# Seven block products in place of eight in half of the chunks of a gate and up projection

## The chip, the core and the metric

The kernel runs on one core of one Trainium2 chip. A core has a matrix engine (TensorE, PE in the rows, with PEld for its weight loads), VectorE (DVE), ScalarE (ACT), GpSimd (POOL) and the DMA queues, SP's among them. The metric is device time in microseconds for one execution; lower is better.

## The reference, cut to what matters

The reference is one layer of a streaming encoder for 256 tokens of width 2048: four token mixers merged by gates, then a feed-forward block (SwiGLU). The change lies in the feed-forward block alone:

```python
h = rms_norm(x, norm_ffn_pre[l])
ffn = (jax.nn.silu(h @ w_gate[l]) * (h @ w_up[l])) @ w_down[l]
x = x + rms_norm(ffn, norm_ffn_post[l])
```

`h` is 256 x 2048, `w_gate` and `w_up` are 2048 x 5632, `w_down` is 5632 x 2048, all float32.

## The kernel before, in words

Each float32 matrix product is computed as three products of rounded operands. Both factors are split into a high part in the engine's float32r format and a low part, the rest; then hi·hi, hi·lo and lo·hi are added up in PSUM. The activations are split once and stay in SBUF with their 2048 features on 16 x 128 partitions (`h2_hi`, `h2_lo`; the trace calls them `h_hi`, `h_lo` or, by their buffers, `hT_hi`, `hT_lo`). The weights stream through.

A weight chunk holds 256 input features and 512 output columns, 512 KB, as a tile of 128 partitions x 2 x 512. `Stream.chunk` (L587 to L601) loads it through SP's queue into one of four `raw` buffers, ScalarE writes the rounded high part `hi` (L599), and VectorE subtracts it from `raw` into `lo` (L600); `hi` and `lo` have three buffers each. These steps carry a raised priority, so that the program's scheduler lets them run ahead of the products.

`gemm_tok` (L645 to L663) takes eight chunks for one group of 512 columns. Each chunk has two halves `k` of 128 features; each of them meets two halves `i` of 128 tokens in three matmuls (L660 to L662), with 128 x 128 activations as the stationary operand and 512 weight columns moving, so 12 matmuls a chunk. The sum for each half of the tokens fills one PSUM bank of 512 columns. The first stages of the kernel use `gemm_feat` (L668 to L682) in its place, where the weights are stationary and 256 activation columns move, 24 matmuls a chunk.

The feed-forward part (L1012 to L1034) runs over 11 groups `g` of 512 columns: the gate product into two banks `bg`, then ScalarE's sigmoid (L1024) and VectorE's scaled product (L1025) out of those banks into `sg`, the up product into two banks `bu`, the multiplication by `bu` (L1028), eight transposes on TensorE into `tq` (L1033) and two copies into `aT` (L1034), from which the down projection reads. In the program, the first operands of the down projection are made by L1043 and L1044 (`ah`, `al`). Each engine takes its instructions in the order in which the scheduler wrote them; a waiting instruction holds up what is queued behind it on its engine. GpSimd has no part in the eleven groups; it issues the load of the gain vector `gain2` (L1016) ahead of them, and elsewhere it writes constants, issues a few loads and computes inverse square roots with a power operation (L157, L337, L379, L643, L729).

Of the kernel before, what the change touches and what calls it, by code (L numbers as in the profile page):

```python
# [6 lines left out]
F32 = mybir.dt.float32  # L7
F32R = mybir.dt.float32r
I32 = mybir.dt.int32
AF = mybir.ActivationFunctionType  # L10
ALU = mybir.AluOpType
AX = mybir.AxisListType
PSUM = bass.MemoryType.PSUM
# [567 lines left out]
class Stream:  # L581


    def __init__(self, e, ring):
        self.e, self.ring = e, ring
# [18 lines left out]
def hybrid_kernel(tc, x, xt, w_l, w_in, w_branch, w_out, w_gate, w_up, w_down, post_mix, post_ffn, wa2_d, w2_d, a2_d, g2_d, lq_d,  # L604
# [9 lines left out]
    with ExitStack() as ctx:  # L614
# [4 lines left out]
        e.dram = ctx.enter_context(tc.tile_pool(name="dr", bufs=1, space=bass.MemoryType.DRAM))  # L619
        mmp = ctx.enter_context(tc.tile_pool(name="mmp", bufs=1, space=PSUM))  # L620
        stream = Stream(e, ring)

        def bank():
            return mmp.tile([128, 512], F32, tag="mm", name="mm", bufs=4)
# [15 lines left out]
        def rms(ssum, n, eps):  # L640

            V.tensor_scalar(ssum, ssum, 1.0 / n, eps, op0=ALU.mult, op1=ALU.add)  # L642
            G.tensor_tensor(ssum, ssum, e.mhalf.to_broadcast(list(ssum.shape)), op=ALU.pow)  # L643

        def gemm_tok(w, lhs, nk, banks, runs={}, into={}):  # L645

# [18 lines left out]
        def columns(w, g):  # L665
            return lambda kc: w[kc, g]
# [345 lines left out]
        with ExitStack() as fctx:  # L1012
            F = fctx.enter_context(tc.tile_pool(name="F", bufs=1))
            aT = F.tile([128, 44, 256], F32, name="aT")
            gain = F.tile([128, 2048], F32, name="gain2")
            nc.gpsimd.dma_start(gain, post_ffn.unsqueeze(0).to_broadcast([128, 2048]))  # L1016
            with tc.tile_pool(name="tq", bufs=1, space=PSUM) as tq:
                for g in range(11):
                    bg, bu = [bank(), bank()], [bank(), bank()]
                    lhs2 = lambda kt: (h2_hi[:, kt], h2_lo[:, kt])  # L1020
                    sg = F.tile([128, 2, 512], F32, tag="sg", name="sg", bufs=2)
                    gemm_tok(columns(w_gate, g), lhs2, 16, bg, {0: 3} if g == 0 else {})
                    for i in range(2):
                        S.activation(sg[:, i], bg[i], AF.Sigmoid, scale=r2[:, i, 0:1])  # L1024
                        V.scalar_tensor_tensor(sg[:, i], bg[i], r2[:, i, 1:2], sg[:, i], op0=ALU.mult, op1=ALU.mult)  # L1025
                    gemm_tok(columns(w_up, g), lhs2, 16, bu)
                    for i in range(2):
                        V.tensor_tensor(sg[:, i], sg[:, i], bu[i], op=ALU.mult)  # L1028
                    for kp in range(2):
                        ps = tq.tile([128, 2, 256], F32, tag="tq", name="tq", bufs=4)  # L1030
                        for k in range(2):
                            for i in range(2):
                                T.transpose(ps[:, k, i * 128:(i + 1) * 128], sg[:, i, (2 * kp + k) * 128:(2 * kp + k + 1) * 128], ident)  # L1033
                        S.copy(aT[:, 4 * g + 2 * kp:4 * g + 2 * kp + 2], ps)  # L1034
            wd = fctx.enter_context(tc.tile_pool(name="wd", bufs=1, space=PSUM))
            fg = F.tile([128, 2, 2048], F32, name="fg")
            sq = F.tile([128, 512], F32, name="sqf", bufs=2)
# [51 lines left out]
            for i in range(2):  # L1089
                with tc.high_priority(offset=e.boost):  # L1090
                    V.tensor_reduce(s1[:, i:i + 1], ssq[:, i], axis=AX.X, op=ALU.add)
                    rms(s1[:, i:i + 1], 2048.0, 1e-6)
                for g in range(4):
                    cs = slice(g * 512, (g + 1) * 512)
                    V.scalar_tensor_tensor(fg[:, i, cs], fg[:, i, cs], s1[:, i:i + 1], x2[:, i, cs], op0=ALU.mult, op1=ALU.add)
                    (nc.sync, nc.scalar)[g % 2 * i].dma_start(outr[:, i, cs], fg[:, i, cs])


class TagPool:
# [67 lines left out]
```

## Time and profile before

| | us |
|---|---|
| median of 3 runs (lowest to highest) | 1647.84 (1646.72 to 1647.86) |
| the profiled execution, device time | 1646.59 |
| its span in the trace | 1644.8 |
| TensorE with a matmul in flight | 1630.7 |
| VectorE busy | 996.4 |
| ScalarE busy | 760.4 |
| GpSimd busy | 33.1 |

Busy times are read against the span, and by stage: the average of the whole span mixes stages with different loads. A matmul's row lasts longer than its place in the stream, since matmuls overlap; the time that one costs is the distance from its start to the next one's. A row's last bracket says how long its engine was idle before it and what ended that.

### The profile page before, as it was taken

Reading aid. Unit: us, or ns where it says so; the run is one execution under the profiler, and the core shown is the slowest. Engines: PE = TensorE matmul, PEld = TensorE weight load, DVE = VectorE, ACT = ScalarE, POOL = GpSimd, SP = SyncE. Lnnn points to the kernel's source line nnn. Section 1 sums busy time; section 2 is a strip of 40 time slices with the busy share of each in tenths; the row PEclk is TensorE's granted clock in tenths of the full one; section 3 lists DMA queues with packets and bytes.
Section 4 is the critical chain, followed back from the end, with each engine's and each line's share of the span. In section 5 each row is a group of like instructions: output and inputs, shape, how many; then the busy total and the mean of one; then the engine's idle time right before and its main releaser. Section 6 shows DMA issues by size and latency. Waiting matters only on the chain.

```text
span 1644.8 us, 21807 instructions
## 1 busy us (share of the span) xinstructions
PE 1630.7 (99%) x8632; PEld 1384.1 (84%) x8632; DVE 996.4 (61%) x1173; ACT 760.4 (46%) x879; POOL 33.1 (2%) x46
## 2 busy tenths in 40 slices
PE   9999999999999999999999999999999999999997
PEld 8999988887889978888888888888888888888886
DVE  7668785669875477555555755554455555556555
ACT  6453443336554355444444644444444444445443
POOL 0000110000000001000000000000000000000000
PEclk9999999999999999999999999999999999999999
DMA  8554565445556545765655555555555555555564
GB/s 296 182 167 145 185 205 177 138 141 166 167 167 193 186 160 182 267 192 190 184 190 203 190 188 188 190 192 189 187 189 190 192 193 189 185 198 188 200 192 141
DMA packets 85974, 306.84 MB, mean 187 GB/s; under 512 B 9584, under 2 KB 11904, under 8 KB 85360
## 3 DMA queue, kind: packets, MB, share of 16 engines
q1 hardware_dynamic: 84208, 298.72, 55.7%
q0 software_dynamic: 1232, 5.95, 1.1%
q8 instruction: 67, 1.10, 0.3%
q10 hardware_dynamic: 432, 0.79, 0.1%
q14 instruction: 35, 0.29, 0.0%
HBM read 302.40 MB, written 3.01 MB: 186 GB/s over the span
## 4 chain that ended last, share of the span: by engine, by line
PE 97%; DVE 1%; issue 1%; DMA 0%; ACT 0%; POOL 0%; DVEq 0%; POOLq 0%; ACTq 0%
PE mm L661 21%; PE mm L662 21%; PE mm L660 21%; PE mm L682 4%; PE mm L680 4%; PE mm L681 4%; PE mm L1055 2%; PE mm L1057 2%; PE mm L1056 2%; PE wd L1057 2%; PE wd L1055 2%; PE wd L1056 2%; PE tq L1033 1%; DVE lo L600 0%; PE ps L464 0%
## 5 line engine op out<-in xcount | busy, mean ns | idle before, releaser
L600 DVE TENSOR_TENSOR lo<-raw,hi 128x1024 fp32r<-128x1024 f32 (+1 forms) x554 | 676.9, 1223 | 552.0 <-ACT hi L599 550.8
L599 ACT CAST hi<-raw 128x1024 fp32r<-128x1024 f32 (+1 forms) x554 | 582.4, 1051 | 723.3 <-PE mm L662 510.3
L661 PE MATMUL mm<-lo,h_hi 128*128 128x512 f32 x704 | 274.9, 390 | 0.0
L662 PE MATMUL mm<-hi,h_lo 128*128 128x512 f32 x704 | 273.9, 390 | 0.1
L660 PE MATMUL mm<-hi,h_hi 128*128 128x512 f32 x704 | 250.6, 391 | 0.2 <-ACT h_hi L360 0.2
L661 PE MATMUL mm<-lo,hT_hi 128*128 128x512 f32 x608 | 238.7, 393 | 0.2 <-DVE lo L600 0.2
L662 PE MATMUL mm<-hi,hT_lo 128*128 128x512 f32 x608 | 237.6, 391 | 0.0
L660 PE MATMUL mm<-hi,hT_hi 128*128 128x512 f32 x608 | 219.7, 392 | 1.9 <-ACT vg L894 1.9
L681 PE MATMUL mm<-hT_lo,hi 128*128 128x256 f32 (+1 forms) x640 | 179.9, 282 | 0.7 <-DVE hT_lo L361 0.7
L682 PE MATMUL mm<-hT_hi,lo 128*128 128x256 f32 (+2 forms) x640 | 178.6, 283 | 1.2 <-DVE lo L600 1.2
L680 PE MATMUL mm<-hT_hi,hi 128*128 128x256 f32 (+1 forms) x640 | 179.7, 283 | 0.0
L660 PEld LDWEIGHTS mm<-hi,h_hi 128*128 128x128 f32 x704 | 132.2, 188 | 27.8 <-ACT h_hi L360 0.9
L662 PEld LDWEIGHTS mm<-hi,h_lo 128*128 128x128 f32 x704 | 132.2, 188 | 27.6 <-DVE s L642 0.5
L661 PEld LDWEIGHTS mm<-lo,h_hi 128*128 128x128 f32 x704 | 132.2, 188 | 27.0
L660 PEld LDWEIGHTS mm<-hi,hT_hi 128*128 128x128 f32 x608 | 114.2, 188 | 26.2 <-ACT vg L894 2.3
L661 PEld LDWEIGHTS mm<-lo,hT_hi 128*128 128x128 f32 x608 | 114.2, 188 | 25.0 <-issue 1.0
L662 PEld LDWEIGHTS mm<-hi,hT_lo 128*128 128x128 f32 x608 | 114.2, 188 | 23.8 <-issue 0.3
L682 PEld LDWEIGHTS mm<-hT_hi,lo 128*128 128x128 f32 (+2 forms) x640 | 119.7, 188 | 2.5 <-DVE lo L600 1.6
L681 PEld LDWEIGHTS mm<-hT_lo,hi 128*128 128x128 f32 (+1 forms) x640 | 120.2, 188 | 1.6 <-DVE hT_lo L361 0.9
L680 PEld LDWEIGHTS mm<-hT_hi,hi 128*128 128x128 f32 (+1 forms) x640 | 119.6, 187 | 1.1 <-issue 0.2
L1057 PE MATMUL mm<-hi,al 128*128 128x512 f32 x168 | 65.4, 389 | 0.0
L1056 PE MATMUL mm<-lo,ah 128*128 128x512 f32 x168 | 65.4, 389 | 0.0
(361 smaller groups left out, 1672.4 us busy)
## 6 DMA issues: line engine op xcount, KB each, us to landing
raw<-in_w_in_dram SPq DMA_DIRECT2D x224, 512.0 KB, 3.5
raw<-in_w_gate_dram SPq DMA_DIRECT2D x88, 512.0 KB, 3.5
raw<-in_w_up_dram SPq DMA_DIRECT2D x88, 512.0 KB, 3.5
raw<-in_w_down_dram SPq DMA_DIRECT2D x88, 512.0 KB, 3.4
raw<-in_w_branch_dram SPq DMA_DIRECT2D x32, 512.0 KB, 3.8
raw<-in_w_out_dram SPq DMA_DIRECT2D x32, 512.0 KB, 3.5
raw<-in_w_l_dram SPq DMA_DIRECT2D x8, 464.0 KB, 7.4
xs<-in_x_dram POOLq DMA_DIRECT2D x1, 2048.0 KB, 12.1
```

What stands on the lines that cost most here:

```text
L599: nc.scalar.copy(hi[:, :, :w], raw[:, :, :w])
L600: nc.vector.tensor_tensor(lo[:, :, :w], raw[:, :, :w], hi[:, :, :w].bitcast(F32), op=ALU.subtract)
L660: mm(banks[i_], ah[:, ts], hi[:, k, :], start=kt == 0, stop=False)
L661: mm(banks[i_], ah[:, ts], lo[:, k, :], start=False, stop=False)
L662: mm(banks[i_], al[:, ts], hi[:, k, :], start=False, stop=kt == nk - 1)
L680: mm(ps, hi[:, k, cs], hT_hi[:, kt, :], start=first, stop=False, skip_group_check=True)
L681: mm(ps, hi[:, k, cs], hT_lo[:, kt, :], start=False, stop=False, skip_group_check=True)
L682: mm(ps, lo[:, k, cs], hT_hi[:, kt, :], start=False, stop=last, skip_group_check=True)
L1033: T.transpose(ps[:, k, i * 128:(i + 1) * 128], sg[:, i, (2 * kp + k) * 128:(2 * kp + k + 1) * 128], ident)
L1055: mm(bk[j][i], ah[:, k, ts], hi[:, k, :], start=kt == 0, stop=False)
L1056: mm(bk[j][i], ah[:, k, ts], lo[:, k, :], start=False, stop=False)
L1057: mm(bk[j][i], al[:, k, ts], hi[:, k, :], start=False, stop=kt == 43)
```

## The change

In the gate and up products four of the eight chunks (numbers 1, 3, 4 and 6) are multiplied in another way; the first gate product stays as it was. Such a chunk is seen as a product of 2 x 2 blocks: two halves of the tokens by two halves of the features, and two halves of the features by two halves of 256 columns. The plain way takes eight block products, Strassen's scheme in Winograd's form takes seven, of sums of the blocks.

- Sums of activation blocks (`Seven.sums`): once, four sums for each of the four chunks, on GpSimd, split into high and low by ScalarE and VectorE.
- Sums of weight blocks (`Seven.chunk`): for each such chunk GpSimd makes four blocks of 256 columns in three additions. ScalarE and VectorE then split seven blocks, three loaded ones and four sums, with two instructions each where there was one.
- The products (`Seven.products`): seven blocks of 256 columns, three matmuls each. Three products fall into one token half's columns alone and are added up in the product's own banks; the other four go to two extra banks `px` and `py`, one buffer each.
- The closing (`Seven.close`): once per product, ScalarE copies a half bank, and five VectorE instructions combine `px` and `py` and add the product's own banks into an SBUF tile `w7` with one buffer. The sigmoid, the scaled product and the multiplication read that tile in place of the banks.
- Room: `tq` has two buffers in place of four, and `gain2`, its load and the pool of the down projection's tiles come after the weight blocks' pool has ended.

The core of the diff:

```diff
+        def gemm_seven(w, lhs, banks, seven):
+            px, py = seven.banks()
+            for kc in range(8):
+                if kc in seven.kcs:
+                    seven.products(kc, lhs, seven.chunk(w(kc)), banks, px, py, kc == seven.kcs[0])
+                    continue
+                hi, lo = stream.chunk(w(kc))
...
+            with tc.high_priority(offset=e.boost):
+                return seven.close(banks, px, py)
...
+                seven = Seven(e, U, tq, (1, 3, 4, 6))
                 for g in range(11):
...
-                    gemm_tok(columns(w_gate, g), lhs2, 16, bg, {0: 3} if g == 0 else {})
+                    if g == 0:
+                        gemm_tok(columns(w_gate, g), lhs2, 16, bg, {0: 3})
+                        zg = bg
+                        seven.sums(h2_hi, h2_lo)
+                    else:
+                        zg = gemm_seven(columns(w_gate, g), lhs2, bg, seven)
...
-                    gemm_tok(columns(w_up, g), lhs2, 16, bu)
+                    zu = gemm_seven(columns(w_up, g), lhs2, bu, seven)
                     for i in range(2):
-                        V.tensor_tensor(sg[:, i], sg[:, i], bu[i], op=ALU.mult)
+                        V.tensor_tensor(sg[:, i], sg[:, i], zu[i], op=ALU.mult)
                     for kp in range(2):
-                        ps = tq.tile([128, 2, 256], F32, tag="tq", name="tq", bufs=4)
+                        ps = tq.tile([128, 2, 256], F32, tag="tq", name="tq", bufs=2)
...
+    def sums(self, h_hi, h_lo):
+        for c, kc in enumerate(self.kcs):
+            t = self.pool.tile([128, 4, 256], F32, tag="t", name="t", bufs=2)
...
+            G.tensor_tensor(h, h_hi[:, 2 * kc:2 * kc + 2].bitcast(F32), h_lo[:, 2 * kc:2 * kc + 2].bitcast(F32), op=ALU.add)
...
+            nc.scalar.copy(self.s_hi[:, c], s)
+            nc.vector.tensor_tensor(self.s_lo[:, c], s, self.s_hi[:, c].bitcast(F32), op=ALU.subtract)
+    def chunk(self, ap):
+        with e.tc.high_priority(offset=e.boost):
+            raw = e.ring.tile([128, 2, 512], F32, tag="raw", name="raw", bufs=e.nraw)
+            nc.sync.dma_start(raw, ap)
+            b = raw.rearrange("p k (c n) -> p (k c) n", c=2)
+            t = self.pool.tile([128, 4, 256], F32, tag="t", name="t", bufs=2)
+            G.tensor_tensor(t[:, 0:2], b[:, 1:3], b[:, 0:1].to_broadcast([128, 2, 256]), op=ALU.add)
+            G.tensor_tensor(t[:, 2], t[:, 0], b[:, 2], op=ALU.add)
+            G.tensor_tensor(t[:, 3], t[:, 2], b[:, 3], op=ALU.add)
+            hi, lo = (self.pool.tile([128, 1920], F32R, tag=n, name=n, bufs=2)[:, 48:1840].rearrange("p (b n) -> p b n", n=256)
+                      for n in ("hi7", "lo7"))
+            for x, o in ((b[:, 1:4], slice(0, 3)), (t, slice(3, 7))):
+                nc.scalar.copy(hi[:, o], x)
+                nc.vector.tensor_tensor(lo[:, o], x, hi[:, o].bitcast(F32), op=ALU.subtract)
+    def products(self, kc, lhs, ch, banks, px, py, first):
...
+        for (ah, al), b, ps, st in ((a(0, 0), 0, px[:, 0], first), (s(1), 5, px[:, 1], False), (s(2), 4, py[:, 0], first),
+                                    (s(0), 3, py[:, 1], False), (a(1, 0), 2, banks[0][:, 256:512], False),
+                                    (s(3), 1, banks[0][:, 0:256], False), (a(1, 1), 6, banks[1][:, 256:512], False)):
+            mm(ps, ah, hi[:, b], start=st, stop=False, skip_group_check=True)
+            mm(ps, ah, lo[:, b], start=False, stop=False, skip_group_check=True)
+            mm(ps, al, hi[:, b], start=False, stop=kc == self.kcs[-1], skip_group_check=True)
+    def close(self, banks, px, py):
+        w = self.pool.tile([128, 5, 256], F32, tag="w7", name="w7", bufs=1)
+        nc.scalar.copy(w[:, 2], px[:, 0])
+        V.tensor_tensor(w[:, 0], w[:, 2], px[:, 1], op=ALU.add)
+        V.tensor_tensor(w[:, 4], w[:, 0], py[:, 0], op=ALU.add)
+        V.tensor_tensor(w[:, 1:4:2], py[:, 1:2].to_broadcast([128, 2, 256]), w[:, 0:5:4], op=ALU.subtract)
+        for i in range(2):
+            o = w[:, 1 + 2 * i:3 + 2 * i].rearrange("p b n -> p (b n)")
+            V.tensor_tensor(o, o, banks[i], op=ALU.add)
```

## Rows read from the trace of the kernel before

**Rows 1.** Page, part 1: engine, busy us (share of span), instructions; last, granted clock by slices.

```profile
PE 1630.7 (99%) x8632; PEld 1384.1 (84%) x8632; DVE 996.4 (61%) x1173; ACT 760.4 (46%) x879; POOL 33.1 (2%) x46
...
PEclk9999999999999999999999999999999999999999
```

**Rows 2.** Page, part 4: shares of the chain that ended last, by engine and line.

```profile
PE 97%; DVE 1%; issue 1%; DMA 0%; ACT 0%; POOL 0%; DVEq 0%; POOLq 0%; ACTq 0%
PE mm L661 21%; PE mm L662 21%; PE mm L660 21%; PE mm L682 4%; PE mm L680 4%; PE mm L681 4%; PE mm L1055 2%; PE mm L1057 2%; PE mm L1056 2%; PE wd L1057 2%; PE wd L1055 2%; PE wd L1056 2%; PE tq L1033 1%; DVE lo L600 0%; PE ps L464 0%
```

**Rows 3.** Busy time by engine, granted clock, DMA in two stretches, two groups each.

```profile
core 0: us, PE busy (x) PEld busy (x) DVE busy (x) ACT busy (x) POOL busy (x), PEclk, DMA share, GB/s
1100.00:1188.86 88.86, 88.86 (x402) 73.67 (x401) 44.43 (x40) 38.20 (x41) 0.00 (x0) 1.00 0.58 189
1188.86:1277.72 88.86, 88.86 (x402) 73.70 (x401) 44.42 (x40) 38.20 (x41) 0.00 (x0) 1.00 0.58 190
```

**Rows 4.** Groups by line in 1100 to 1188.9: count, busy us, mean ns, idle before, releaser.

```profile
L600 DVE TENSOR_TENSOR lo<-raw,hi 128x1024 fp32r<-128x1024 f32 x32 | 39.2, 1225 | 43.5 <-ACT hi L599 43.5
...
L599 ACT CAST hi<-raw 128x1024 fp32r<-128x1024 f32 x33 | 34.8, 1055 | 46.8 <-PE mm L662 46.8
```

**Rows 5.** Timeline, VectorE: start us, us, engine, line, operation [idle before, releaser].

```profile
1388.90 1.23 DVE L600 TENSOR_TENSOR lo<-raw,hi 128x1024 fp32r<-128x1024 f32 x1 [1.50 <-ACT hi L599]
...
1391.62 1.23 DVE L600 TENSOR_TENSOR lo<-raw,hi 128x1024 fp32r<-128x1024 f32 x1 [1.50 <-ACT hi L599]
...
1394.34 1.23 DVE L600 TENSOR_TENSOR lo<-raw,hi 128x1024 fp32r<-128x1024 f32 x1 [1.49 <-ACT hi L599]
...
1395.48 1.28 DVE L1028 TENSOR_TENSOR sg<-sg,mm 128x512 f32<-128x512 f32 x2
...
901.50 1.41 DVE L971 SCALAR_TENSOR_TENSOR acc<-mg,s,xs 128x512 f32<-128x512 f32 x2 [0.69 <-POOL s L643]
```

**Rows 6.** Timeline, VectorE, first stage (256-column products); then that stretch's busy times.

```profile
65.40 1.23 DVE L600 TENSOR_TENSOR lo<-raw,hi 128x1024 fp32r<-128x1024 f32 x1 [1.60 <-ACT hi L599]
68.22 1.23 DVE L600 TENSOR_TENSOR lo<-raw,hi 128x1024 fp32r<-128x1024 f32 x1 [1.60 <-ACT hi L599]
71.05 1.23 DVE L600 TENSOR_TENSOR lo<-raw,hi 128x1024 fp32r<-128x1024 f32 x1 [1.60 <-ACT hi L599]
73.88 1.23 DVE L600 TENSOR_TENSOR lo<-raw,hi 128x1024 fp32r<-128x1024 f32 x1 [1.60 <-ACT hi L599]
...
63.00:103.00 40.00, 40.00 (x342) 40.00 (x342) 23.02 (x24) 15.40 (x16) 0.00 (x0) 1.00 0.60 193
```

**Rows 7.** Down projection's operand, 512 elements: count, ns min/median/max, first and last start.

```profile
L1043 ACT CAST ah<-aT x44: 610/624/633, 958.1 to 1619.7; 128x512 fp32r<-128x512 f32 x44
L1044 DVE TENSOR_TENSOR al<-aT,ah x44: 684/693/693, 958.8 to 1620.9; 128x512 fp32r<-128x512 f32 x44
```

**Rows 8.** Groups on GpSimd: power operations and memsets, count, busy us, mean ns.

```profile
L379 POOL TENSOR_TENSOR hst<-hst,mhalf 128x4 f32<-128x4 f32 x4 | 4.9, 1234 | 286.0 <-DVE hst L378 286.0
L157 POOL TENSOR_TENSOR rn<-rn,mhalf 128x16 f32<-128x16 f32 x1 | 2.9, 2912 | 98.3 <-DVE rn L156 98.3
...
L265 POOL MEMSET N<- 32x512 f32 x2 | 1.1, 536 | 0.0
L244 POOL MEMSET NN<- 64x1024 f32 x1 | 1.0, 972 | 0.0
```

**Rows 9.** Timeline around the four power operations L379, GpSimd and VectorE.

```profile
465.76 1.01 POOL L379 TENSOR_TENSOR hst<-hst,mhalf 128x4 f32<-128x4 f32 x1 [109.70 <-DVE hst L378]
...
471.01 1.01 POOL L379 TENSOR_TENSOR hst<-hst,mhalf 128x4 f32<-128x4 f32 x1 [4.25 <-DVE hst L378]
471.09 1.23 DVE L600 TENSOR_TENSOR lo<-raw,hi 128x1024 fp32r<-128x1024 f32 x1 [0.15 <-ACT hi L599]
...
627.03 1.22 DVE L600 TENSOR_TENSOR lo<-raw,hi 128x1024 fp32r<-128x1024 f32 x1
...
627.20 1.92 POOL L379 TENSOR_TENSOR hst<-hst,mhalf 128x4 f32<-128x4 f32 x1 [155.18 <-DVE hst L378]
...
645.97 1.01 POOL L379 TENSOR_TENSOR hst<-hst,mhalf 128x4 f32<-128x4 f32 x1 [16.85 <-DVE hst L378]
```

**Rows 10.** Timeline at the start of the gate products.

```profile
920.42 0.48 DVE L361 SCALAR_TENSOR_TENSOR h_lo<-ps,vec,h_hi 128x256 fp32r<-128x256 f32 x1
...
927.43 0.58 POOL L1016 DMA_DIRECT2D gain<-in_post_ffn_dram  x1 [21.76 <-PE mm L662]
...
929.67 0.69 ACT L1024 ACTIVATE sg<-mm,r 128x512 f32<-128x512 f32 x1 [1.49 <-PE mm L662]
```

## What I expected, written before the result was known

> **What bounds the kernel now.** I read the page's busy times first [rows 1]. The matmul engine has work in flight for 99% of the span, VectorE for 61%, GpSimd for 2%, and the granted clock stands at nine tenths or more in every slice. Busy matmuls alone prove little, because they overlap one another, so the chain of what ended last comes next [rows 2]: 97% of it is TensorE, and the three lines that multiply one weight chunk (L660 to L662) hold 63 to 64% of the span. Then the stage that the change touches, gate and up, in two equal stretches of two column groups, four products each [rows 3]. Both give 88.86 us, 22.2 us for one product of eight chunks, with TensorE busy throughout, the clock at 1.00 (its upper level, 2.4 GHz), VectorE at 44.4 us and ScalarE at 38.2 us of 88.86, and GpSimd doing nothing at all. VectorE's idle time there is spent waiting for ScalarE's high parts, and ScalarE's for TensorE to free a buffer [rows 4]: both run ahead and are held back by TensorE. So TensorE's stream sets the time, and any microsecond off it counts while the other engines keep up.
>
> **What TensorE saves.** A chunk today is 12 products of 512 columns, and the split of one chunk follows that of the chunk before it by 2.72 us (1388.90 to 1391.62 to 1394.34) [rows 5]. In the new form it is 7 block products of 3 matmuls, 21 of 256 columns. Matmuls of exactly that shape fill the first stage, 24 to a chunk, and the chunks follow each other there by 2.826 us (65.40, 68.22, 71.05, 73.88) [rows 6], 0.1178 us a matmul. 21 of them take 2.473 us, 0.247 us less than 2.72. The new form is used for four chunks in each of 21 products (11 groups, gate and up, without the first gate): 84 x 0.247 = 20.7 us. The narrow matmul gives back part of the eighth: at half of 2.72/12, 0.1133 us, it would have been 28.6 us. The transposes stay. A product would then take TensorE 22.2 - 4 x 0.247 = 21.2 us.
>
> **What the other engines gain in work.** Seven weight blocks are now split, three as loaded and four summed, 1792 elements a partition in place of 1024. On VectorE 1024 elements take 1.225 us and 512 take 0.693 us [rows 4, 7], so 1.04 ns an element; one behind the other 1024 occupy it for 1.14 us (from 1394.34 to the next start at 1395.48) [rows 5], and 768 would occupy it for 0.87. Per product: 4 x 1.14 for the plain chunks, 4 x (1.14 + 0.87) for the new ones, and 2 x 0.67 for the gating (mean of 0.64, half of the 1.28 us for two, and 0.70, half of the 1.41 us of two scaled additions) [rows 5] = 13.9 us. The closing adds two operations of 256 elements and three of 512, at 0.37 and 0.64 us: 2.7 us. VectorE reaches 16.6 us of 21.2. ScalarE, at 1.055 us for 1024 and 0.63 for 512 [rows 4, 7], so 0.84 for 768, goes to 4 x 1.055 + 4 x 1.90 + about 1.7 for the activation, copies and closing = 13.5 us. Loads keep their bytes, and go from 512 KB in 2.72 us to 512 KB in about 2.6. None of this would bind.
>
> **The unknown cost is the weight sums on GpSimd.** Per chunk three additions of 512, 256 and 256 elements, waited for by ScalarE and VectorE, which split the sums. No addition on GpSimd stands in the trace. Its memset writes 64 x 1024 in 0.972 us and 32 x 512 in 0.536 [rows 8], 0.85 ns an element and 0.1 us to start. One such stream per element gives 1.17 us a chunk, two give 2.04, three (two reads and a write, one after the other) 2.91; the power operation on the same engine, 0.14 us an element (2912 against 1234 ns for 16 and 4), is the far end and would be 143 us a chunk. I leave that end out of the range since its time rises with each value while an addition moves data like the memset does. Between two and three streams, nearest to the memset, I take 2.5 us: 9.9 us per product, 11.6 as the upper bound, 4.7 as the lower. Alone, GpSimd too stays under 21.2.
>
> **Why it does not stay alone.** Four power operations of 128 x 4 on GpSimd take 1.01 us three times and 1.92 us once [rows 9]. In the one at 627.20 VectorE was inside a split with two inputs in SBUF (627.03 to 628.25); counted back from its end at 629.12, the usual 1.01 us starts at 628.11, when VectorE was about through. The other three began with VectorE idle. So a GpSimd read waited for a two-input VectorE operation to finish. In the other direction nothing shows: a split that started 0.08 us behind a power operation took its usual 1.23 us (471.01, 471.09), but that operation reads only a few values and then computes. An addition reads to its end. If the two exclude each other, a product needs their sum: 13.9 us of VectorE (all splits and both gating operations would have both inputs in SBUF) and 9.9 us of GpSimd, 23.8 us. The closing operations, with one input in PSUM, can run beside GpSimd; I count a quarter of their 2.7 us as not hidden, as the raw ring gives GpSimd work to do meanwhile: 24.5 us, over the 22.2 of today. TensorE would then wait for weights: 21 x 2.3 = 48 us.
>
> The Trainium skill (SBUF — State Buffer, Who interferes with whom) speaks against this change in the same place: a VectorE instruction with two SBUF inputs contends with a GpSimd instruction that reads SBUF, and it calls the shared ports an exclusive lock for the whole instruction. By that rule the sum stands as just made, and without it the gain does; the late operation at 627.20 agrees, and the undelayed split at 471.09 shows that the lock is not held once the reads are over.
> The Trainium skill (GPSIMD Engine Reference, section 3.1) gives 4497 ns for an addition of 2048 float32 elements on GpSimd; scaled to 1024 elements that is an estimate of 2.25 us a chunk, and the product would be 23.6 us in place of 24.5. No run here shows it yet.
>
> **Small terms, once each.** The activation sums (four sets, about 1024 elements and five instructions each, some 2.7 us a set) can start when the last low part of the activations is written, about 920.9, and the first is wanted by the second chunk of the first up product, about three us after the first gate's evacuation begins at 929.67 [rows 10]: the first sets fit, and the later sets are wanted later. I count 2 us, up to 5. At the end the first operands of the down projection take memory that the weight blocks leave; the last chunk, a plain one of 2.72 us, hides a copy of 0.63 and a subtraction of 0.69 [rows 7]. If they lay on the closing's memory instead, the cost would be some 4 us. The gain vector's load moves behind the stage on GpSimd's queue, 0.58 us to issue [rows 10], and is first read after the 22 chunks of the down projection's first half: nothing. Transpose buffers go from four to two, and the next eight transposes are half of 88.86 us away: nothing. The two extra banks must be free by the next product's second chunk, 5.4 us behind the last new one; the reads take about 1.8 us unless VectorE is late.
>
> **Sum and rivals.** The profiled execution took 1646.6 us, its span 1644.8 and 1.8 around it; the median of the runs is 1.2 above that. **A, the shared port binds:** 1646.6 + 48 + 2 = 1697, as a median 1698. Its own range: with two streams on GpSimd and all closing hidden a product takes 22.1 us, nothing lost (1650 with the small terms); with three streams and no closing hidden 28.2, or + 126 us (1775). For it: 627.20, and that VectorE's two-input work fills two thirds of the new product. Against: one occurrence, and spans on GpSimd are rough. **B, TensorE stays the bound:** 1646.6 - 20.7 + 2 = 1628, as a median 1629, down to 1621 at the shorter pitch. It holds where GpSimd waits only at its start and then runs beside VectorE, or where an addition costs one stream (13.9 + 4.7 = 18.6 us, under 21.2). For it: VectorE's undelayed splits. **C, the weight loads come to light:** each matmul has its own load of 0.188 us; if the new blocks' addresses keep two loads from overlapping, a chunk takes 21 x 0.188 = 3.95 us, + 1.23 x 84 = 103 us, 1750. It decides from a pitch over 0.13 us. Against: the first stage keeps 0.1178 us with the loads in flight 40.00 of 40.00 us [rows 6].
>
> **How the numbers follow.** A 0.60, of which 0.06 ends within 0.2%; B 0.34, of which 0.01 does; C 0.06. A measurement of this kernel can tell about 0.2%, 3.3 us, from no change. Faster 0.33, same 0.07, slower 0.60. The likeliest is A, 1698, with 1650 to 1775 as its own range; the range over both signs reaches into B and leaves out about a tenth at either end: 1624 to 1765.
>
> **What would show it.** By A: a gate or up product lasts about 24.5 us instead of 22.2, TensorE idles for low parts or sums, VectorE's two-input operations or GpSimd's additions last longer than alone, and the two engines' busy times of a product add up to nearly its length. By B: about 21.2 us, TensorE without idle, additions overlapping splits at their usual 1.23 us. By C: starts over 0.13 us apart inside a new chunk. I am wrong about the size if an addition costs far less than 2.5 us a chunk, and about the sign if it runs beside the splits.

## The result: slower by 2.5%, for two reasons in place of one

| | before | after |
|---|---|---|
| median, us (lowest to highest) | 1647.85 (1646.72 to 1647.87) | 1687.75 (1685.93 to 1690.45) |
| ratio (95% interval) | | 1.0247 (1.0234 to 1.026) |
| span of the profiled execution | 1644.8 | 1686.4 |

The page of the kernel after: busy times, granted clock by slices, chain of what ended last [rows 1, 2].

```profile
PE 1630.9 (97%) x9388; PEld 1411.6 (84%) x9388; DVE 1210.3 (72%) x1366; ACT 824.6 (49%) x988; POOL 400.9 (24%) x318
...
PEclk9999999999999999999999899999999999999999
...
PE 70%; DVE 11%; issue 7%; POOL 6%; DMA 4%; ACT 1%; DVEq 0%; POOLq 0%; SPq 0%; ACTq 0%
```

TensorE no longer carries the chain alone: VectorE, GpSimd and transfers hold a fifth of it, and one slice of the clock shows 8.

Where the 41.6 us of span lie can be read from one instruction, the gate's sigmoid. Its starts, from the view of its line: `sg<-mm` is the first group (plain gate), `sg<-w` the ten others, two instructions each.

```profile
L1048 ACT ACTIVATE sg<-w,r x20: 706/717/726, 1001.3 to 1416.7; 128x512 f32<-128x512 f32 x20
L1048 ACT ACTIVATE sg<-mm,r x2: 682/686/689, 933.0 to 933.5; 128x512 f32<-128x512 f32 x2
```

The last group's first sigmoid starts 0.7 us ahead of the 1416.7. So the first evacuation begins at 933.0 in place of 929.7 [rows 10], + 3.3 us; from there to the second group 68.3 us pass, against 43.9 in the kernel before, + 24.4; the nine intervals behind it take 46.08 us each, against 44.44, + 1.64 each or + 14.8; what follows gives 0.9 back. **The changed kernel pays more once, at the start (some 28 us), than in its nine steady groups (15 us).** A product takes 23.0 us in these, with 22.2 before.

Busy times by stretch in the kernel after: the start, then two spans of two groups each (columns as in [rows 3]).

```profile
937.00:980.00 43.00, 31.35 (x171) 26.91 (x171) 27.67 (x24) 17.13 (x20) 34.53 (x34) 0.84 0.38 122
1093.33:1185.56 92.23, 86.65 (x545) 76.93 (x544) 83.97 (x77) 49.84 (x61) 67.48 (x49) 1.00 0.54 183
1185.56:1277.60 92.04, 87.50 (x546) 78.36 (x545) 84.18 (x77) 50.04 (x60) 67.86 (x49) 0.98 0.55 183
```

In a steady pair of groups TensorE has nothing in flight for some 5 us, VectorE shows 84 us of 92 and GpSimd 68. What these two engines are busy with, in 1093.33 to 1185.56 of the kernel after (count, busy us, mean ns, idle before):

```profile
L1174 DVE TENSOR_TENSOR lo<-t,hi 128x1024 fp32r<-128x1024 f32 x16 | 24.9, 1557 | 7.7 <-ACT hi L1173 7.7
L600 DVE TENSOR_TENSOR lo<-raw,hi 128x1024 fp32r<-128x1024 f32 x16 | 24.0, 1501 | 0.0
L1174 DVE TENSOR_TENSOR lo<-raw,hi 128x768 fp32r<-128x768 f32 x16 | 18.6, 1165 | 0.0
L1203 DVE TENSOR_TENSOR w<-w,mm 128x512 f32<-128x512 f32 x9 | 5.8, 675 | 0.0
L1049 DVE SCALAR_TENSOR_TENSOR sg<-w,r,sg 128x512 f32<-128x512 f32 x4 | 4.7, 1226 | 0.0
...
L1168 POOL TENSOR_TENSOR t<-t,raw 128x256 f32<-128x256 f32 x16 | 24.3, 1520 | 1.3
L1167 POOL TENSOR_TENSOR t<-raw 128x512 f32<-128x512 f32 x17 | 23.1, 1359 | 22.2 <-DMA raw<-in_w_gate_dram 11.5 <-DMA raw<-in_w_up_dram 10.8
L1169 POOL TENSOR_TENSOR t<-t,raw 128x256 f32<-128x256 f32 x16 | 21.8, 1363 | 1.3
```

The split L600 was 1225 ns [rows 4] and is 1501 now, and an addition of 256 elements (L1168) takes more than one of 512 (L1167): these are waits inside an instruction, not work. The closing's L1203, which has one input in PSUM, takes 675 here and 681 in a run without these reads (E1 below). The timeline shows how (VectorE, then GpSimd, same stretch; start us, us):

```profile
1102.07 0.95 DVE L1174 TENSOR_TENSOR lo<-raw,hi 128x768 fp32r<-128x768 f32 x1
1102.94 1.21 DVE L1174 TENSOR_TENSOR lo<-t,hi 128x1024 fp32r<-128x1024 f32 x1
1104.18 1.93 DVE L1174 TENSOR_TENSOR lo<-raw,hi 128x768 fp32r<-128x768 f32 x1
...
1103.24 2.05 POOL L1167 TENSOR_TENSOR t<-raw 128x512 f32<-128x512 f32 x1 [5.92 <-DMA raw<-in_w_gate_dram]
1105.38 1.33 POOL L1168 TENSOR_TENSOR t<-t,raw 128x256 f32<-128x256 f32 x1
1106.79 0.74 POOL L1169 TENSOR_TENSOR t<-t,raw 128x256 f32<-128x256 f32 x1
1107.48 1.30 POOL L1167 TENSOR_TENSOR t<-raw 128x512 f32<-128x512 f32 x1
```

Undisturbed, the additions take 1.30, 0.74 and 0.74 us (L1167 and L1169 in the last two rows, L1168 at 970.79). The addition at 1103.24 meets a split that runs to 1104.15 and takes 2.05; the split at 1104.18 meets that addition and takes 1.93 in place of 0.95; the addition at 1105.38 meets that split and takes 1.33 in place of 0.74. Each waits for the other. The Trainium skill (SBUF — State Buffer, Who interferes with whom) calls the two engines' shared ports an exclusive lock; the trace agrees, in both directions.

At the start GpSimd's queue is the sight to see (kernel after: the semaphore waits of GpSimd's sequencer at the line of the first sum; VectorE by time; GpSimd by time):

```profile
L1145 POOLq EVENT_SEMAPHORE  x2: 43/10889/21735, 906.0 to 927.8; - x2
...
927.58 0.15 DVE L1027 TENSOR_REDUCE r<-ssq 128x1 f32<-128x4 f32 x1
...
927.95 3.58 POOL L1145 TENSOR_TENSOR t<-h_hi,h_lo 128x512 f32<-128x512 f32 x2 [21.32 <-issue]
931.49 1.43 POOL L644 TENSOR_TENSOR r<-r,mhalf 128x2 f32<-128x2 f32 x1
...
943.69 0.86 POOL L1150 TENSOR_TENSOR t<-t 128x128 f32<-128x128 f32 x2
945.60 2.86 POOL L1167 TENSOR_TENSOR t<-raw 128x512 f32<-128x512 f32 x2 [1.04 <-DVE s_lo L1152]
```

The first sum is held from 906.0 until VectorE's last reduction for the norm (L1027) ends at 927.73. All four sets of activation sums run ahead of the first weight sum, from 927.95 to 944.55, and `r`, which the first sigmoid reads, is queued behind their first two instructions. The waits of 932 to 1001 name the victims (total us, times, longest):

```profile
ACT hi L1173 <- POOL t L1169: 17.8, 5, 5.2
...
PE px L1187 <- ACT hi L1173: 10.2, 2, 9.8
...
PE mm L1187 <- ACT s_hi L1151: 2.6, 1, 2.6
ACT sg L1048 <- POOL r L644: 2.4, 1, 2.4
```

TensorE waits 9.8 us for a cast, which waits for the weight sums. Part of the start is TensorE's clock: in the stretch of 937 to 980, of which TensorE idles 11.7 us, it is 0.84, so partly at the lower level of 1.2 GHz, and matmuls of 256 columns last 0.41 us there (at 952.01) in place of 0.28.

### The profile page after: what moved, and what is told of

It is laid out like the page before. It is cut to its first block, busy times and chain, and to the rows that moved or that the text cites. A ratio compares the mean times of both kernels' runs of the same rounds, so it can differ in the third digit from the quotient of the medians.

```text
span 1686.4 us, 24050 instructions
## 1 busy us (share of the span) xinstructions
PE 1630.9 (97%) x9388; PEld 1411.6 (84%) x9388; DVE 1210.3 (72%) x1366; ACT 824.6 (49%) x988; POOL 400.9 (24%) x318
## 4 chain that ended last, share of the span: by engine, by line
PE 70%; DVE 11%; issue 7%; POOL 6%; DMA 4%; ACT 1%; DVEq 0%; POOLq 0%; SPq 0%; ACTq 0%
PE mm L680 12%; PE mm L681 12%; PE mm L682 12%; PE mm L702 4%; PE mm L700 4%; PE mm L701 4%; DVE lo L600 4%; DVE lo L1174 3%; PE mm L1082 2%; PE mm L1084 2%; PE mm L1083 2%; PE wd L1084 2%; PE wd L1082 2%; PE wd L1083 2%; DMA raw<-in_w_up_dram 2%
## 5 line engine op out<-in xcount | busy, mean ns | idle before, releaser
L600 DVE TENSOR_TENSOR lo<-raw,hi 128x1024 fp32r<-128x1024 f32 (+1 forms) x470 | 597.4, 1272 | 337.5 <-ACT hi L599 335.9
L599 ACT CAST hi<-raw 128x1024 fp32r<-128x1024 f32 (+1 forms) x470 | 493.3, 1050 | 572.9 <-PE mm L682 275.3
L1174 DVE TENSOR_TENSOR lo<-t,hi 128x1024 fp32r<-128x1024 f32 x84 | 134.0, 1596 | 42.6 <-ACT hi L1173 42.6
L1167 POOL TENSOR_TENSOR t<-raw 128x512 f32<-128x512 f32 x84 | 116.2, 1385 | 110.2 <-DMA raw<-in_w_up_dram 54.2
L1173 ACT CAST hi<-t 128x1024 fp32r<-128x1024 f32 x84 | 88.0, 1049 | 99.2 <-POOL t L1169 99.1
L660 PE MATMUL mm<-lo,h_hi 128*128 128x512 f32 x336 | 131.6, 392 | 0.0
L659 PE MATMUL mm<-hi,h_hi 128*128 128x512 f32 x336 | 131.1, 391 | 0.0
L661 PE MATMUL mm<-hi,h_lo 128*128 128x512 f32 x336 | 128.3, 391 | 0.0
L1168 POOL TENSOR_TENSOR t<-t,raw 128x256 f32<-128x256 f32 x84 | 125.8, 1499 | 6.1
L1169 POOL TENSOR_TENSOR t<-t,raw 128x256 f32<-128x256 f32 x84 | 113.5, 1352 | 6.1
```

Of the source, the lines that this page charges most:

```text
L599: nc.scalar.copy(hi[:, :, :w], raw[:, :, :w])
L600: nc.vector.tensor_tensor(lo[:, :, :w], raw[:, :, :w], hi[:, :, :w].bitcast(F32), op=ALU.subtract)
L659: mm(banks[i], ah[:, ts], hi[:, k, :], start=kt == 0, stop=False, skip_group_check=True)
L660: mm(banks[i], ah[:, ts], lo[:, k, :], start=False, stop=False, skip_group_check=True)
L661: mm(banks[i], al[:, ts], hi[:, k, :], start=False, stop=kt == 15, skip_group_check=True)
L1174: nc.vector.tensor_tensor(lo[:, o], x, hi[:, o].bitcast(F32), op=ALU.subtract)
```

## The experiments

Theory P: in the steady groups the two engines' reads exclude each other and TensorE waits for what they make. Theory S: the start is a cost of its own, from GpSimd's queue. Rivals: the longer way of a chunk (load, sums, two casts, two splits) with its buffers, whatever the ports do; VectorE's own added work; weight loads (C of the prediction). Every edit is against the kernel after; with lines inserted, later line numbers shift by a few. "Start" is the interval from the first to the second group's sigmoid, "group" the mean of the nine behind it, both read as above from the one profiled execution (in E3 the slowest of its runs, 1675.58, in E10 the fastest, 1646.52); the kernel before has 43.9 and 44.44. They are times on ScalarE: TensorE can already be at the next product when a sigmoid starts.

| run | median us | ratio to before (95%) | start | group |
|---|---|---|---|---|
| after | 1687.75 | 1.0247 (1.0234 to 1.026) | 68.3 | 46.08 |
| e1_write_only | 1643.75 | 0.9973 (0.9963 to 0.9984) | 59.0 | 42.20 |
| e2_no_weight_sums | 1632.06 | 0.9903 (0.9889 to 0.9918) | 50.2 | 41.97 |
| e3_first_up_plain | 1670.95 | 1.0147 (1.013 to 1.0163) | 53.6 | 46.20 |
| e4_two_chunks | 1689.46 | 1.0254 (1.0239 to 1.0269) | 50.0 | 48.44 |
| e5_two_write_only | 1641.94 | 0.997 (0.9958 to 0.9981) | 47.0 | 43.62 |
| e6_vector_sums | 1669.9 | 1.0133 (1.0115 to 1.0152) | 56.7 | 45.27 |
| e7_vector_sums_three | 1646.37 | 0.9995 (0.9986 to 1.0004) | 48.5 | 44.00 |
| e8_vector_sums_two | 1661.51 | 1.0091 (1.0076 to 1.0106) | 45.3 | 46.17 |
| e9_three_more_raw | 1667.38 | 1.0124 (1.0109 to 1.0139) | 49.8 | 46.29 |
| e10_two_more_raw | 1650.63 | 1.0029 (1.0018 to 1.0039) | 43.6 | 44.26 |
| e11_two_gpsimd_more_raw | 1641.14 | 0.9969 (0.9956 to 0.9982) | 45.6 | 43.53 |
| e12_three_gpsimd_more_raw | 1640.29 | 0.9959 (0.9945 to 0.9972) | 48.9 | 43.10 |

**E1: GpSimd keeps its place and about its length, but hardly reads.** VectorE, ScalarE, TensorE and SP have the same instructions in the same order as in the kernel after.

```diff
-            G.tensor_tensor(t[:, 0:2], b[:, 1:3], b[:, 0:1].to_broadcast([128, 2, 256]), op=ALU.add)
...
+            G.memset(t, 0.5)
+            G.tensor_tensor(t[:, 0, 0:2], b[:, 1, 0:2], b[:, 0, 0:2], op=ALU.add)
+            G.memset(t[:, 1:4], 0.25)
...
```

> Leaves out the weight sums: on GpSimd each of the three additions of a chunk is a memset (1024, 768 and 512 elements a partition, about as long as the additions alone) and an addition of 2 elements that reads the raw block, so that the summed blocks arrive as late and the raw buffers are held as long, but GpSimd hardly reads. Theory of the shared port: the splits on VectorE return to 1.22 us, a column group of gate and up falls from 46.0 us to 42.4 to 43.5, and the time from 1687.8 to 1650 to 1662 (10 groups, 2.5 to 3.6 us each; the slow start of the stage stays). Rival, latency (raw buffers held until GpSimd is done, so that loads and splits come late): a group stays at 45.5 to 46.5 us and the time within 5 us of 1688.

1643.75, and a group falls from 46.08 to 42.20. Groups by line in 1100 to 1188, then busy times of 87 us of the steady part, of E1:

```profile
L600 DVE TENSOR_TENSOR lo<-raw,hi 128x1024 fp32r<-128x1024 f32 x17 | 20.9, 1226 | 6.5 <-ACT hi L599 6.3
L1177 DVE TENSOR_TENSOR lo<-t,hi 128x1024 fp32r<-128x1024 f32 x17 | 20.8, 1226 | 0.4 <-ACT hi L1176 0.4
L1177 DVE TENSOR_TENSOR lo<-raw,hi 128x768 fp32r<-128x768 f32 x17 | 16.2, 956 | 8.7 <-ACT hi L1176 8.7
L1167 POOL MEMSET t<- 128x1024 f32 x17 | 16.3, 957 | 32.0 <-DVE lo L1177 32.0
...
1079.00:1166.00 87.00, 87.00 (x559) 78.85 (x558) 70.60 (x78) 53.30 (x62) 50.98 (x97) 1.00 0.64 199
```

GpSimd is busy 51.0 us there, more than the 44.5 that two groups' additions take undisturbed (16 x 2.78), and every split is back at its own length; TensorE is busy throughout. The chain of buffers and the order are those of the kernel after, so the rival of the longer way falls, and P stands for the steady part. Of the start's 24.4 us 9.3 go as well, but it is still 59.0: S is another matter.

**E2: no weight sums at all.** The casts and splits read the loaded chunk twice.

```diff
-            G.tensor_tensor(t[:, 0:2], b[:, 1:3], b[:, 0:1].to_broadcast([128, 2, 256]), op=ALU.add)
...
-            for x, o in ((b[:, 1:4], slice(0, 3)), (t, slice(3, 7))):
+            for x, o in ((b[:, 1:4], slice(0, 3)), (b, slice(3, 7))):
```

> Leaves out the weight sums altogether: the four summed blocks are split from the raw blocks, with the same work for TensorE, VectorE and ScalarE and none for GpSimd but the activation sums. Theory of the shared port: TensorE is the bound again, a group takes 42.4 us (2 products of 21.2), and the time is 1645 to 1655; what stays over the 1629 that TensorE alone would give is the slow start of the stage. Rival, VectorE's own added work (16.6 us a product and waits on TensorE in its queue) is what binds: a group stays over 45 us and the time over 1675.

1632.06, below what was expected, as the start shrank too (50.2). The scheduler also wrote another order for VectorE and ScalarE, yet eight of the nine intervals take 42.2 us, as in E1 (the first takes 40.1, which lowers the mean). This is what TensorE allows. One new chunk and the plain one behind it (timeline of TensorE, first matmul of each chunk; start us):

```profile
1107.90 0.28 PE L1183 MATMUL px<-hi,h_hi 128*128 128x256 f32 x1
...
1110.37 0.39 PE L659 MATMUL mm<-hi,h_hi 128*128 128x512 f32 x1
...
1113.09 0.28 PE L1183 MATMUL px<-hi,h_hi 128*128 128x256 f32 x1
```

2.47 us for the new form, 2.72 for the plain one: weight loads stay hidden.

**E3: only the first up product goes back to plain chunks.**

```diff
-                    zu = gemm_seven(columns(w_up, g), lhs2, bu, seven)
+                    if g == 0:
+                        gemm_tok(columns(w_up, g), lhs2, 16, bu)
+                        zu = bu
+                    else:
+                        zu = gemm_seven(columns(w_up, g), lhs2, bu, seven)
```

> The first up product also stays in the plain form, so that the activation sums have 22 us more before they are wanted; 4 of the 84 new chunks are given up (1 us on TensorE). Theory: of the 68.3 us between the first and the second gate's evacuation 22 are waiting for activation sums and for the weight sums queued behind them on GpSimd, and go: 1664 to 1670, the group of the later ones still 46.0. Rival, the first new product costs its price wherever it stands, since the first weight sums meet an empty lead: the waiting moves to the second gate, 1680 to 1688.

The start falls from 68.3 to 53.6 and the time by 17 us; the steady groups stay at 46.2. S is confirmed as to place. What makes up the rest, 53.6 in place of 43.9, isn't settled: in that stretch TensorE has nothing in flight for only 3.1 us, at a clock of 0.97, while ScalarE waits 14.9 us for GpSimd's sums.

**E4: half as many new chunks**, the first up product plain as in E3.

```diff
-                seven = Seven(e, U, tq, (1, 3, 4, 6))
+                seven = Seven(e, U, tq, (3, 6))
```

> As the run with the first up product plain, with two new chunks a product (3 and 6) in place of four: 40 in all. Theory of the shared port: VectorE's two-input time falls to 12.2 us a product and GpSimd's to about 5.4, together 17.6, under TensorE's 21.7; TensorE binds and the time is 1646.6 - 40 x 0.247 = 1637 to 1641, faster than before. Rival, every new chunk costs a wait of its own whatever else there is (the 1.6 us a group over the kernel before, and the 2 us a group not gained, by half): a group of 45.2 us, 1653 to 1657.

A clear miss, 1689.46. The two engines' shared work is only 17.8 us a product by undisturbed durations (VectorE 6 x 1.14 + 2 x 2.01 + 1.34 = 12.2, GpSimd 2 x 2.78 = 5.6), TensorE's 21.7, and yet a group takes 48.44. Three views of E4: around 1151 to 1159, TensorE, VectorE and GpSimd by time; then the granted clock in two stretches of it, and busy times of 87 us of the steady part.

```profile
1151.45 0.44 PE L1061 MATMUL tq<-ident,sg 128*128 128x128 f32 x2 [1.05 <-DVE sg L1056]
...
1153.66 0.50 PE L660 MATMUL mm<-lo,h_hi 128*128 128x512 f32 x1 [1.42 <-DVE lo L600]
...
1157.00 0.63 PE L660 MATMUL mm<-lo,h_hi 128*128 128x512 f32 x1
...
1151.31 2.30 DVE L600 TENSOR_TENSOR lo<-raw,hi 128x1024 fp32r<-128x1024 f32 x1
...
1151.14 1.39 POOL L1171 TENSOR_TENSOR t<-raw 128x512 f32<-128x512 f32 x1 [5.14 <-DMA raw<-in_w_gate_dram]
```

```profile
1151.00:1155.00 4.00, 1.97 (x9) 1.28 (x10) 4.00 (x4) 1.78 (x2) 3.70 (x3) 0.95 0.06 14
1155.00:1159.00 4.00, 4.00 (x17) 3.47 (x17) 4.00 (x4) 3.15 (x5) 0.33 (x1) 0.63 0.75 243
...
1079.00:1166.00 87.00, 82.11 (x423) 69.79 (x422) 64.54 (x60) 39.63 (x48) 29.33 (x21) 0.96 0.53 176
```

A weight sum starts the moment its load lands (1151.14) and doubles the split that TensorE waits for next (2.30 us); TensorE idles 2 of 4 us, and in the next 4 us, though busy throughout, is granted 0.63 of 2.4 GHz on average, so part of them at the lower level of 1.2, with matmuls of 512 columns at 0.63 us in place of 0.39.

**E5: E4 with memsets in place of the additions** (three of 1024 elements, and additions of two), the order of E4 but for one place at the start.

```diff
-            G.tensor_tensor(t[:, 0:2], b[:, 1:3], b[:, 0:1].to_broadcast([128, 2, 256]), op=ALU.add)
...
+            G.memset(t[:, 0:4], 0.5)
+            G.tensor_tensor(t[:, 0, 0:2], b[:, 1, 0:2], b[:, 0, 0:2], op=ALU.add)
...
```

> Two new chunks a product as before (3 and 6, first up plain, 1689 us, 48.4 us a group), but GpSimd's three additions are each a memset of 1024 elements and an addition of 2 elements that reads the raw block; leaves out the weight sums. The order of the instructions on every engine is that of the run with two chunks, but for one place at the start of the stage, and GpSimd's part takes rather longer than the additions alone. Theory, the shared port also explains the run with two chunks: an addition makes one split late by up to 1.3 us where TensorE has no lead left, though the sums of busy times (17.6 of 21.7 us) leave room: a group falls to 43.5 to 45 us and the time to 1638 to 1655. Rival, the order of the instructions in the queues (closing and gating ahead of the next splits, loads just in time) makes TensorE wait, port or not: a group stays over 47 us and the time over 1675.

1641.94, a group 43.62, with GpSimd busier than in E4 (104 of 261 us, against 93). Groups by line in 1100 to 1188 and 87 us of the steady part of E5:

```profile
L600 DVE TENSOR_TENSOR lo<-raw,hi 128x1024 fp32r<-128x1024 f32 x24 | 29.2, 1222 | 6.3 <-ACT hi L599 6.3
...
1079.00:1166.00 87.00, 87.00 (x474) 75.41 (x473) 60.88 (x68) 43.87 (x52) 35.40 (x48) 1.00 0.58 193
```

So E4's loss comes from the reads as well, although the sum of the loads left 4 us of room a product. The sum alone can't be what decides.

**E6: four chunks, the weight sums on VectorE**, first up product plain. E7 and E8 have three and two such chunks.

```diff
-            G.tensor_tensor(t[:, 0:2], b[:, 1:3], b[:, 0:1].to_broadcast([128, 2, 256]), op=ALU.add)
+            e.nc.vector.tensor_tensor(t[:, 0:2], b[:, 1:3], b[:, 0:1].to_broadcast([128, 2, 256]), op=ALU.add)
...
```

> As the run with the first up product plain (four new chunks, 1671 us, 46.0 us a group), with the three weight additions of each chunk on VectorE in place of GpSimd: 0.64 + 0.37 + 0.37 = 1.4 us a chunk, 5.5 a product. VectorE then has 16.6 + 5.5 = 22.1 us of work a product and GpSimd none. Theory, with the port free the sum is VectorE's own: it binds over TensorE's 21.1, a group takes 44.2 to 45.5 us, the time 1650 to 1665, better than on GpSimd. Rival, GpSimd's help is worth having in spite of the port, VectorE is now the longer path: a group over 46 us, over 1672.

1669.9, level with E3 and between the two forecasts; a group, 45.27, is where the theory had it. VectorE alone is then busy 94% of the steady part, and no operation is prolonged (L600 at 1220 ns). That VectorE sets the pace is argued: ScalarE also waits for loads, 66 us in 330.

> Three new chunks a product (1, 3, 6) with the sums on VectorE, first up plain. VectorE 19.9 us a product, TensorE 21.4. Theory: TensorE binds, 1646.6 - 20 x 3 x 0.247 = 1632, up to 1640 with local waits; faster than before. Rival, at over nine tenths VectorE has no lead over TensorE where the closing stands in its queue: 1645 to 1660.

Chunks `(1, 3, 6)`: 1646.37, no difference from before that could be told; that is in the rival's range.

> Two new chunks a product (2 and 5) with the sums on VectorE, first up plain. VectorE 17.7 us a product, TensorE 21.7. Theory: TensorE binds, 1646.6 - 40 x 0.247 = 1637, up to 1642. Rival, as with two chunks on GpSimd the closing and the gating keep a split waiting in VectorE's queue once a group: 1655 or more.

Chunks `(2, 5)`: 1661.51, worse than three although VectorE does less: in 330 us it waits 81 us for loads (lines of the sums, by releaser), and TensorE for L600. Its sums stand in the same queue as the splits, and a sum that waits for its load holds the next split up. That load has to go through the ring of four `raw` buffers, in turn with the plain chunks.

**E9 to E11: two `raw` buffers of their own for the new chunks**, on E7, E8 and E4; the unused tail of two tiles pays for them.

```diff
-            raw = e.ring.tile([128, 2, 512], F32, tag="raw", name="raw", bufs=e.nraw)
+            raw = self.pool.tile([128, 2, 512], F32, tag="raw7", name="raw7", bufs=2)
...
-            hi, lo = (self.pool.tile([128, 1920], F32R, tag=n, name=n, bufs=2)[:, 48:1840].rearrange("p (b n) -> p b n", n=256)
+            hi, lo = (self.pool.tile([128, 1840], F32R, tag=n, name=n, bufs=2)[:, 48:1840].rearrange("p (b n) -> p b n", n=256)
```

> As the run with three new chunks and the sums on VectorE (1646 us, a group 44.3 us), with two raw buffers of their own for the new chunks, six raw buffers in all. In that run VectorE waited 33 us in 330 for loads. Theory: the loads come late because a raw buffer is held until VectorE's last sum and split; with two more TensorE binds, a group takes 43 to 43.5 us and the time is 1632 to 1640. Rival, VectorE's queue order (closing, gating and sums ahead of splits) holds TensorE up: a group stays at 44 to 44.5 us and the time within 4 us of 1646.

1667.38, worse than E7 by 21 us, where neither forecast had it. The scheduler wrote another order, and which wait of it costs the 21 us is not settled.

> As the run with two new chunks and the sums on VectorE (1661 us, a group 46 us), with two raw buffers of their own for the new chunks. Theory: late loads made that run slow, 81 us of VectorE's waiting in 330: 1637 to 1645. Rival, the queue order: within 5 us of 1661.

1650.63, between the two forecasts and 11 us better than E8; VectorE's waiting for loads falls from 81 to 48 us in 330. So the loads seem a part of it, though the order changed here too.

> As the run with two new chunks and the sums on GpSimd (1689 us, a group 48.4 us), with two raw buffers of their own for the new chunks. Theory, collisions at the port cost TensorE time only as far as the lead is too short to take them in, and the loads that come just in time keep it short: with six raw buffers a group falls to 44 to 46 us, 1640 to 1665. Rival, the collisions cost the same with any lead: over 1680.

1641.14, 48 us better than E4 and faster than before. Groups by line in 1100 to 1188, waits of 1079 to 1339 and two groups' busy times of E11:

```profile
L600 DVE TENSOR_TENSOR lo<-raw,hi 128x1024 fp32r<-128x1024 f32 x25 | 36.0, 1452 | 15.0 <-ACT hi L599 15.0
...
L1172 POOL TENSOR_TENSOR t<-t,raw 128x256 f32<-128x256 f32 x8 | 10.7, 1339 | 0.6
...
ACT hi L599 <- PE mm L661: 88.9, 66, 2.8
...
1079.00:1166.00 87.00, 87.00 (x474) 75.36 (x473) 71.85 (x68) 45.15 (x53) 33.13 (x24) 1.00 0.60 192
```

The collisions are all there still (1452 ns for L600, as against 1382 in E4), and TensorE is busy throughout at full clock. In E4 the longest waits of the same stretch between two engines were for GpSimd:

```profile
ACT hi L1177 <- POOL t L1173: 48.0, 21, 2.9
```

In E11 it is ScalarE that waits for TensorE: the weights are ready ahead of need, and a collision eats lead instead of TensorE's time. The buffers didn't change alone: with them the scheduler put the new chunks' loads and casts ahead of plain ones. Which of the two gives the lead wasn't separated.

**E12: E11 with three chunks**, `(1, 3, 6)`, where the shared work comes to 13.1 + 3 x 2.78 = 21.4 us a product, TensorE's to 21.5.

> Three of the eight chunks of a group (1, 3 and 6) go through seven products, the weight sums on GpSimd, the first up projection in plain chunks, and two raw buffers of their own for the chunks that wait for GpSimd, so that GpSimd can run further ahead. Per product the shared-port work is VectorE's two-input operations (about 13 us) and GpSimd's sums (3 x 2.78 = 8.3 us), 21.4 in sum; TensorE needs 21.5 (22.2 less three times 0.247). Theory that collisions cost TensorE only where GpSimd and VectorE have no lead: the lead covers them, a group takes 43 to 43.6 us, 1632 to 1641 us. Rival that the port's sum sets the pace once it reaches TensorE's: a group takes over 44.4 us and the time is 1645 to 1665.

1640.29, and a group takes 43.10. Groups by line in 1100 to 1188 and 87 us of the steady part of E12:

```profile
L600 DVE TENSOR_TENSOR lo<-raw,hi 128x1024 fp32r<-128x1024 f32 x21 | 30.9, 1470 | 6.6 <-ACT hi L599 6.6
...
L1171 POOL TENSOR_TENSOR t<-raw 128x512 f32<-128x512 f32 x13 | 23.6, 1818 | 34.9 <-DMA raw<-in_w_up_dram 22.6 <-DMA raw<-in_w_gate_dram 12.4
...
1066.00:1153.00 87.00, 87.00 (x516) 77.26 (x515) 76.93 (x73) 48.77 (x59) 53.80 (x36) 1.00 0.63 194
```

TensorE is busy throughout. The steady groups win 0.43 us each over E11; the start costs 3.3 us more (48.9 against 45.6), presumably since there GpSimd still has more to do ahead of the second gate. So the two kernels' intervals overlap; both beat the kernel before and the changed one. Four chunks with such buffers weren't tried.

## Why the prediction was right, and where it was not

The forecast was + 50 us and slower; + 40 came. The mechanism holds, and two terms of the sum are off in opposite directions.

- **What bounds, and what TensorE saves: right.** A new chunk takes 2.47 us as summed. Freed of the weight sums' reads, a group takes 42.20 us (E1, and all but the first interval of E2), 0.26 less than 44.44 - 8 x 0.247; that quarter of a microsecond is not settled. Case B's 1629 is what E2 shows nearly (1632.06, with a start 6 us longer than that of before).
- **The other engines' work doesn't bind by itself: right.** In E1 VectorE shows 70.6 us of 87, ScalarE 53.3.
- **The price of the sums: a little low.** 2.5 us a chunk were taken, 2.78 came (1.30 + 0.74 + 0.74), inside the bounds. The Trainium skill (GPSIMD Engine Reference, section 3.1) gave the estimate of 2.25; here three smaller additions took 0.53 more.
- **The two engines exclude each other: right**, and the half that rested on one row [rows 9] is shown in both directions: E1 takes away the reads alone and 3.9 us a group go with them.
- **The size of that: the step that was mis-sized.** The sum of the two engines' durations was to give 24.5 us a product, and 23.0 came: 21 x 0.8 = 17 us in place of 48. With the measured 2.78 it would have been 25.7. Adding whole durations counts their ends twice: in the three handovers of the timeline of 1102.94 to 1106.71 the next instruction's undisturbed length, counted back from its end, begins 0.16, 0.13 and 0.14 us ahead of the other's end. Twelve additions a product have 24 such ends at most, or 3.4 us by this estimate, so 22.3 to 25.7. The quarter of the closing that I counted as not hidden couldn't be read off, and neither could the sign that the two busy times add up to a product's length: waits inside instructions count as busy, 84 and 67 us in 92.
- **The start: the step that failed.** I counted 2 us, up to 5, as "the first sets fit, and the later sets are wanted later". The sums began 7 us later than the 920.9 that I had assumed, at 927.95. That 920.9 was misread: in the trace of before one more low part is written, from 923.91 to 924.39. And the first sum waited for L1027, as its semaphore row shows; in all thirteen runs with such sums it starts 0.22 us after that reduction ends, and in the kernel before the gain vector's load stood in GpSimd's queue behind the same one, until 926.82. Which data that wait protects, the trace doesn't say. The sums took 16.6 us, `r`'s 1.4 among them, where four times 2.7 were worked out; and, what I had not looked at, GpSimd takes its queue in order, so that all four sets stood ahead of the first weight sum (945.60), which TensorE wanted at about 933, and the first two instructions ahead of `r`. The cost was 22 us over a steady group, of which E3 gives back 15 by leaving only the first up product plain, and 3.3 at the first evacuation. How much of it is the queue's order and how much the collisions and the clock wasn't separated; E1 takes 9 us off the start by taking the weight sums' reads away.
- **C: wrong, as expected.** A new chunk of E2 takes 2.47 us, 0.118 us a matmul, where C wanted over 0.13.
- **The remaining small terms** (down projection's operands, gain vector, transposes, two banks) show no cost together: from the last gate's sigmoid on the changed kernel takes 0.9 us less, though that sigmoid's place behind its product also differs.

So 1698 was near by luck of two errors: the steady loss was a third of what I worked out, and the start cost ten times as much.

## What to carry to other kernels

An offload to GpSimd is priced by what its reads do to VectorE's operations with two inputs in SBUF and they to it, and by how far ahead of the bounding engine both run; the sum of busy times tells only whether the lead can be kept. What is computed once ahead of a steady loop is a stage of its own: list what stands in the same queue behind it and when the bounding engine wants that first. With fewer chunks, buffers of their own and a plain first product the same scheme wins 0.4%.

## What the runs showed of the hardware that I had not expected

- The lock works against both sides, and an addition of 256 elements suffers most in proportion: 0.74 us alone, 1520 ns on average beside VectorE. GpSimd's memsets next to the same splits cost these nothing (1226 ns in E1). The Trainium skill (SBUF — State Buffer, Who interferes with whom) says that a GpSimd instruction which only writes doesn't contend; E1 and E5 agree.
- Short waits cost twice. In E4 TensorE idled 1.05 and 1.42 us within a few microseconds, and the granted clock of the following 4 us was 0.63; over 87 us it was 0.96. Of the 4.8 us that a group of E4 takes more than one of E5, idle time accounts for some 2.5 (13.4 of 261 us). The mean granted clock of these 261 us, 0.97 where E5 has 1.00, accounts for some 1.5 more by estimate; the other 0.8 is open.
- Half the added work gave a worse time (E4 against E3, 48.44 and 46.20 us a group). The reading that where a load arrives just in time for the sum that hangs on it, the moment matters more than the amount of work, is supported by E11, though the order changed with its buffers.
